# Layer 0's feed-forward network in one pass: seven block products for the latent tokens, down sums per F-tile

## The chip, the core and the metric

The kernel runs on one core of a Trainium2 chip. A core has a matrix engine (PE, whose weight loads the profile lists as PEld), a vector engine (DVE), a scalar engine (ACT), a general engine (POOL) and a queue engine (SP) that issues nearly all DMAs here. Each engine works through its own instructions in program order; semaphores make one wait for another. The metric is device time in microseconds of one execution; three executions of the kernel before gave 1770.62, 1772.52 and 1773.2.

## The reference

Two layers act on 512 latent rows `x` and 256 context rows `ctx`, D = 1024, in fp32. What matters here is the second half of layer 0, for both streams:

```
mx = s_c @ mod_w[l] + mod_b[l]           # six parts of 1024: shift, scale, gate, twice
gate, up = jnp.split(h @ w_in, 2, axis=-1)        # w_in: 1024 x 5632
swiglu   = (jax.nn.silu(gate) * up) @ w_out       # w_out: 2816 x 1024
x   = x   + gx2 * swiglu(rms(x)   * (1 + scx2) + shx2)
ctx = ctx + gc2 * swiglu(rms(ctx) * (1 + scc2) + shc2)
```

The hidden width 2816 is 22 F-tiles of 128. Layer 1 does the same for the latent rows alone, after its own attention.

## The kernel before, in words

**Every product is three.** An fp32 operand is split into a high part in the PE's format (an ACT cast) and a rest (a DVE or POOL subtraction); hi·hi, hi·lo and lo·hi are summed in PSUM.

**Layer 0's FFN** is `ffn`, from 427.9 us of the trace, its last down product at 1003.9 us. It takes the F-tiles in pairs. Per F-tile, gate and up each run over 8 K-tiles of 128 and three passes, and each of these 48 steps is one matmul over the 512 latent columns and one over the 256 context columns (L814, in `half`). ACT takes Silu of the gate (L842), DVE multiplies it by the up (L844), ACT and DVE split the result (L445, L446). Weights arrive raw by SP in two buffers, ACT casts them (L334) and DVE subtracts (L335). The down product of a pair is twelve groups (6 row tiles of 128 by 2 halves of 512 columns), each six matmuls into one of four PSUM banks (L869 to L871). After each group `residual` multiplies the bank by the gate row (L439) and adds it to the rows (L440), both on DVE. The last four F-tiles' downs are done together at the end.

**Layer 1's modulation** (24 chunks of 256 columns for one or two streams, 32 chunk-and-stream units in all) is worked out in the same stretch, by `mod_chunks_by_pool`: ACT scales the raw weights (L213), POOL adds them up (L214 to L219), and PE sums over partitions: a row product per unit (`modrow`, L224) and small products that turn the rows into columns (`modcol`, L232).

**Layer 1's FFN** is already done in blocks (`ffn_by_blocks`): the 512 latent columns and the K dimension are halved, and seven products of quarter size, each 12 matmuls of 256 columns, stand in the place of eight, with sums of weight blocks on POOL ahead and sums of results on DVE behind. All its instructions are recorded through one helper, so the trace gives them one line, L886. It sums each pair's down groups in four banks.

**Order.** In layer 0's `ffn` a scheduler places the instructions; it slips down groups between the gate and up matmuls. In the block code the instructions keep program order on each engine (`Pinned`).

Of the kernel before, what the change touches and what calls it, by code (L numbers as in the profile page):

```python
# [18 lines left out]
P = 128  # L19
# [18 lines left out]
MODS1 = (2, 2, 2, 2, 2, 3, 3, 4, 4, 0)  # L38
# [3 lines left out]
C_N = C_S4 + 4  # L42
# [21 lines left out]
def backbone(es: ExitStack, tc: tile.TileContext, x, c, ctx, c_ctx, mod_w, mod_b, norm_mix_w, norm_ffn_w,  # L64
# [132 lines left out]
    def mod_chunks_by_pool(chunks, pool):  # L197

        width = 256
        all_accs = []  # L200
        for l, part, n, streams in chunks:
            c0 = part * D + n * width
            accs = [pool.tile([P, width], F32, name="ma", tag="ma", bufs=4) for _ in range(streams)]
            for pc in range(2):
                w = pool.tile([P, 4, width], F32, name="modw", tag="mw", bufs=2)
                nc.sync.dma_start(
                    w, mod_w[l, pc * 4 * P:(pc + 1) * 4 * P, c0:c0 + width].rearrange("(j p) n -> p j n", p=P))
                for i, acc in reversed(list(enumerate(accs))):

                    pr = pool.tile([P, 4, width], F32, name="modp", tag="mp", bufs=1) if i else w  # L210
                    for k in range(4):
                        kk = 8 * i + 4 * pc + k
                        nc.scalar.activation(pr[:, k], w[:, k], AF.Copy, scale=cols[:, kk:kk + 1])  # L213
                    nc.gpsimd.tensor_add(pr[:, 0:2], pr[:, 0:2], pr[:, 2:4])  # L214
                    if pc == 0:
                        nc.gpsimd.tensor_add(acc, pr[:, 0], pr[:, 1])
                    else:
                        nc.gpsimd.tensor_add(pr[:, 0], pr[:, 0], pr[:, 1])
                        nc.gpsimd.tensor_add(acc, acc, pr[:, 0])  # L219
            all_accs.extend(accs)  # L220
        ps = tr_tile("modrow", [P, width])

        for j, acc in enumerate(all_accs):
            nc.tensor.matmul(ps[32 * j:32 * j + 32, :], cst[:, C_ONE:C_ONE + 32], acc, start=True, stop=True,  # L224
                             tile_position=(0, 32 * j))
# [1457 lines left out]
```

## Time and profile before

| | |
|---|---|
| median of three executions | 1772.52 us |
| profiled execution | 1773.26 us, its span 1771.4 us |
| mean granted PE clock | 0.99 |
| PE busy in the span | 1696.1 us (96%) |
| DVE, ACT, POOL busy | 1066.9, 852.4, 822.4 us |
| layer 0's FFN, first gate matmul to last down | 427.9 to 1003.9 us |

Times within the profile are microseconds from the start of the span. A group row gives line, engine, operation, what it writes and reads, shape and count; then total busy time and mean ns of one; then idle time ahead of it and what ended it. A row of the timeline gives start, length, engine, line and operation, and in brackets the engine's idle time before it and its releaser. [...]

### The profile page before, as it was taken

The page shows a single profiled execution, that of the slowest core. Times are in us where ns is not written, and L with a number is a line of the kernel's source. Part 1 is how long each engine was busy: PE and PEld are TensorE (multiplying, and loading weights), DVE is VectorE, ACT ScalarE, POOL GpSimd, SP SyncE. Part 2 cuts the span into 40 slices and gives each one's busy share as a digit, 9 for nine tenths or more (in the row PEclk, how much of TensorE's full clock was granted, in tenths as well). Part 3 has the DMA queues.
Part 4 walks back from the last instruction along what each step waited for, and adds up shares of the span by engine and source line. Part 5 has one row for each costly group of instructions (what it writes and reads, how often), then busy time and mean ns, then how long its engine had stood idle before and what let it go on. Part 6 is the DMA issues. An engine that isn't in the chain of part 4 may idle for free. (4 is left out here: it accounts for less than half of the span.)

```text
span 1771.4 us, 28187 instructions
## 1 busy us (share of the span) xinstructions
PE 1696.1 (96%) x10606; PEld 1471.0 (83%) x10606; DVE 1066.9 (60%) x1891; ACT 852.4 (48%) x1841; POOL 822.4 (46%) x1087
## 2 busy tenths in 40 slices
PE   6999999989999999999999999999988999999998
PEld 3887777767888888888888889999986798999997
DVE  4776555444365565554552665666664478877777
ACT  6556565443354444433332466666664345444441
POOL 2753333422054443312230657767772247777770
PEclk8999999999999999999999999999998999999999
DMA  9212233303443334433332211111122325333332
GB/s 319 55 43 73 84 96 108 107 25 119 143 144 97 105 108 155 131 110 108 105 119 62 94 37 36 37 36 51 43 84 83 96 72 161 92 95 107 107 96 95
DMA packets 176168, 169.96 MB, mean 96 GB/s; under 512 B 16608, under 2 KB 162592, under 8 KB 176032
## 3 DMA queue, kind: packets, MB, share of 16 engines
q1 hardware_dynamic: 175680, 167.96, 30.8%
q8 instruction: 83, 1.36, 0.3%
q14 instruction: 53, 0.43, 0.1%
q10 hardware_dynamic: 352, 0.21, 0.0%
HBM read 161.82 MB, written 6.32 MB: 95 GB/s over the span
## 5 line engine op out<-in xcount | busy, mean ns | idle before, releaser
L432 PE MATMUL inps<-wih,hT 128*128 128x384 f32 x384 | 132.9, 346 | 2.1 <-ACT qkv L630 2.0
L439 DVE TENSOR_TENSOR dps<-dps,g 128x512 f32<-128x512 f32 x128 | 87.8, 696 | 72.0 <-PE dps L871 57.6
L434 PE MATMUL inps<-wih,hT 128*128 128x384 f32 x384 | 130.8, 341 | 0.0
L433 PE MATMUL inps<-wil,hT 128*128 128x384 f32 x384 | 130.7, 340 | 0.0
L814 PE MATMUL pg<-hT,wgh 128*128 128x512 f32 x352 | 129.8, 392 | 0.0
L814 PE MATMUL pu<-hT,wuh 128*128 128x512 f32 x352 | 129.4, 391 | 0.4 <-DVE x L440 0.4
L213 ACT ACTIVATE modw<-modw,cols 128x256 f32<-128x256 f32 x192 | 82.0, 498 | 84.1 <-DMA modw<-in_mod_w_dram 80.4
L869 PE MATMUL dps<-wdh,hdh 128*128 128x512 f32 x264 | 106.3, 404 | 1.6 <-DVE x L440 1.6
L870 PE MATMUL dps<-wdl,hdh 128*128 128x512 f32 x264 | 104.5, 396 | 0.0
L871 PE MATMUL dps<-wdh,hdl 128*128 128x512 f32 x264 | 101.8, 396 | 0.0
L214 POOL TENSOR_TENSOR modw<-modw 128x512 f32<-128x512 f32 x48 | 62.1, 1294 | 84.5 <-ACT modw L213 84.5
L814 PE MATMUL pg<-hTc,wgh 128*128 128x256 f32 x352 | 98.1, 282 | 2.7 <-ACT hTc L308 2.4
L814 PE MATMUL pu<-hTc,wuh 128*128 128x256 f32 x352 | 97.8, 282 | 0.0
L321 POOL TENSOR_TENSOR wil<-wir,wih 128x256 fp32r<-128x256 f32 x84 | 68.2, 839 | 62.7 <-ACT wih L334 50.0
L886 PE MATMUL pg<-hT,wbh 128*128 128x256 f32 (+1 forms) x464 | 88.6, 288 | 1.6 <-DVE pg L886 1.6
L886 POOL TENSOR_TENSOR wbl<-ws,wbh 128x256 fp32r<-128x256 f32 x72 | 58.8, 847 | 64.2 <-PE pu L886 54.3
L440 DVE TENSOR_TENSOR x<-x,dps 128x512 f32<-128x512 f32 x128 | 85.2, 682 | 2.3
L552 ACT ACTIVATE Pt<-sc,nm 128x256 f32<-128x256 f32 (+3 forms) x96 | 68.0, 712 | 38.1 <-DVE nm L548 14.7
L886 POOL TENSOR_TENSOR ws<-wr 128x256 f32<-128x256 f32 x72 | 77.1, 1092 | 12.6 <-DMA wr<-in_ffn_w_in_dram 12.6
L886 PEld LDWEIGHTS pg<-hT,wbh 128*128 128x128 f32 x464 | 74.0, 188 | 6.2 <-DVE pg L886 1.8
L814 PEld LDWEIGHTS pg<-hT,wgh 128*128 128x128 f32 x352 | 66.0, 188 | 14.9 <-ACT sg L842 0.4
L814 PEld LDWEIGHTS pu<-hT,wuh 128*128 128x128 f32 x352 | 66.0, 188 | 14.9 <-issue 0.8
(332 smaller groups left out, 5507.1 us busy)
## 6 DMA issues: line engine op xcount, KB each, us to landing
modw<-in_mod_w_dram SPq DMA_DIRECT2D x96, 512.0 KB, 4.4
wdr<-in_ffn_w_out_dram SPq DMA_DIRECT2D x44, 512.0 KB, 3.7
wr<-in_ffn_w_in_dram SPq DMA_DIRECT2D x44, 512.0 KB, 5.2
wir<-in_od_w_in_dram SPq DMA_DIRECT2D x96, 128.0 KB, 2.3
wgr<-in_ffn_w_in_dram SPq DMA_DIRECT2D x22, 512.0 KB, 4.3
wur<-in_ffn_w_in_dram SPq DMA_DIRECT2D x22, 512.0 KB, 3.5
x<-in_x_dram SPq DMA_DIRECT2D x8, 512.0 KB, 6.8
wir<-in_ev_w_in_dram SPq DMA_DIRECT2D x16, 256.0 KB, 2.7
```

Of the source, the lines that this page charges most:

```text
L213: nc.scalar.activation(pr[:, k], w[:, k], AF.Copy, scale=cols[:, kk:kk + 1])
L321: nc.gpsimd.tensor_sub(lo[c], raw[c], hi[c])
L432: nc.tensor.matmul(ps, hs[0][:, k, :], a, start=k == 0, stop=False)
L433: nc.tensor.matmul(ps, hs[0][:, k, :], b, start=False, stop=False)
L434: nc.tensor.matmul(ps, hs[1][:, k, :], a, start=False, stop=k == KT - 1)
L439: nc.vector.tensor_mul(tmp, ps, g[:, n * 512:(n + 1) * 512])
L440: eng.tensor_add(xt[:, n * 512:(n + 1) * 512], xt[:, n * 512:(n + 1) * 512], tmp)
L814: nc.tensor.matmul(ps[:, s0:s1], a, cols_T(b, s0, s1)[:, k, :], start=k == 0 and q == 0, stop=k == KT - 1 and q == 2)
L869: nc.tensor.matmul(ps, hh, a, start=j == 0, stop=False)
L870: nc.tensor.matmul(ps, hh, b, start=False, stop=False)
L871: nc.tensor.matmul(ps, hl, a, start=False, stop=j == nj - 1)
L886: return tc.keep_in_program_order(op(*args, **kw))
```

## The change

Layer 0's FFN becomes `ffn_mixed`, one pass over F-tiles.

- **The first two F-tiles** stay conventional. Meanwhile SP writes all rows to DRAM (the latent ones into the output buffer), and DVE and POOL form the sums of activation blocks. ACT copies this pair's down sums over the rows in SBUF, so that the rows then hold bare sums of the down products.
- **F-tiles 2 to 21** use seven block products of 12 matmuls for the latent tokens (`product`, `four`: `r2`, `r1`, `r3`, `a11`, `a12`, `a22`, `r4`), and 48 matmuls of 256 columns for context's gate and up (`gate_up`).
- **Down sums** are made per F-tile: twelve groups of three matmuls over three banks in turn (`acc0`, `acc1`, `tr0`), each followed by one DVE add into the rows. In tile f stand groups 0 to 7 of tile f-1 and groups 8 to 11 of tile f-2. The fourth bank, `tr1`, holds context's gate and up and the modulation's sums. The last three F-tiles' downs end the pass, with the gate on the sum of all.
- **Gate and rows** come in at the end: tiles 20 and 21 make the gate rows through DRAM, `resumed` multiplies the sums by the gate and adds the rows read back.
- **Layer 1's modulation**: 16 pairs of units, one per tile from tile 4 to 19: four raw loads (`load`), 16 scalings (`scale`), six POOL adds (`sum`), four row matmuls (`rows`), two column matmuls (`columns`). The raw tiles share two buffers with the raw down weights.

All of it from tile 2 on is pinned to program order, under one line, L761. Product, silu, split and gating are as before; the engines' orders ahead of this FFN are unchanged, and in layer 1 ACT, DVE and POOL rows shift a little in the attention. The core of the diff (the sums for the weights, the generators for this layer's own gate part, the end cases of tiles 20 and 21, and the closing of memory pools are left out):

```diff
-MODS1 = (2, 2, 2, 2, 2, 3, 3, 4, 4, 0)
...
-    def mod_chunks_by_pool(chunks, pool):
...
-    def ffn(l, xs, ntok, wp, fp, done, mods=()):
...
+    def ffn_mixed(xs, w_down, w_up, fp, turn_over, new_rows, done):
...
+        def hidden(f, s0, s1, gate, up, sg):
+            hi, lo = (z[:, s0:s1] for z in hid[f])
+            act.activation(sg, gate, AF.Silu)
+            yield
+            dve.tensor_mul(up, sg, up)
+            act.copy(hi, up)
+            yield
+            dve.tensor_sub(lo, up, f32(hi))
...
+        def down_bank(name="dps"):
+            nonlocal bank
+            bank = (bank + 1) % 3
+            return p_1.tile([P, 512], F32, name=name, tag=("acc0", "acc1", "tr0")[bank])
+
+        def group(fs, t, n, keep=False):
+            ps = down_bank()
+            for f in fs:
+                down_part(ps, f, t, n, f == fs[0], f == fs[-1])
+            yield
+            acc = xs[t][:, n * 512:(n + 1) * 512]
+            if keep:
+                act.copy(acc, ps)
+            else:
+                dve.tensor_add(acc, acc, ps)
+
+        def groups(fs, k0, k1, keep=False):
+            some = [group(fs, t, n, keep) for t, n in order[k0:k1]]
+            for g in some:
+                next(g)
+            return some
...
+            def split_last(self):
+                self.t4 = b12
+                act.copy(b12[0], self.f4)
+                dve.tensor_sub(b12[1], self.f4, f32(b12[0]))
...
+        names = ("r2", "r1", "r3", "a11", "a12", "a22", "a21", "r4")
...
+        def hi():
+            if todo:
+                w, n = todo.pop(0)
+                w.w[n] = [blocks.tile([P, half, P], F32R, name="wb" + z, tag="wb" + z, bufs=9) for z in "hl"]
+                act.copy(w.w[n][0], getattr(w, n))
+                made.append((w.w[n], getattr(w, n), n in ("r1", "r2")))
+
+        def lo():
+            if made:
+                (h, t), raw, by_pool = made.pop(0)
+                if by_pool:
+                    for k in range(0, half, 2):
+                        pool.tensor_sub(t[:, k:k + 2], raw[:, k:k + 2], f32(h)[:, k:k + 2])
+                else:
+                    dve.tensor_sub(t, raw, f32(h))
...
+        class Tile:
+
+            def __init__(self, f, w):
+                self.f, self.w = f, w.w
+                self.ps = [banks.tile([P, SEQ], F32, name=n, tag=n) for n in ("pu", "pg")]
+                (self.e, self.b), (self.a, self.c) = ((p[:, :cols], p[:, cols:]) for p in self.ps)
...
+            def four(self):
+                self.quv = three()
+                self.q, self.u, self.v = (self.quv[:, i * cols:(i + 1) * cols] for i in range(3))
+                act.copy(self.q, self.a)
+                dve.tensor_add(self.u, self.b, self.q)
+                dve.tensor_add(self.v, self.c, self.u)
+                dve.tensor_add(self.b, self.e, self.v)
+                dve.tensor_add(self.u, self.e, self.u)
+
+            def gate_up(self, up):
+                if not up:
+                    self.both = tr_tile("cgu", [P, 2, ctx_cols], one=1)
+                for k, n in enumerate(("a21", "a22") if up else ("a11", "a12")):
+                    product(self.both[:, up], self.w[n], ctx_rows[k], k == 0, k == 1)
...
+            def __init__(self):
+                self.pairs = [[(part, n, i) for i in range(2)] for part in range(2) for n in range(4)] + \
+                    [[(part, n + i, 0) for i in range(2)] for part in range(2, 6) for n in (0, 2)]
+                self.now, self.before, self.loads = None, None, []
...
+            def load(self):
+                if self.now:
+                    part, n, _ = self.now[len(self.loads) // 2]
+                    pc, c0 = len(self.loads) % 2, part * D + n * 256
+                    w = raw_tile([P, 4, 256], "modw")
+                    nc.sync.dma_start(
+                        w, mod_w[1, pc * 4 * P:(pc + 1) * 4 * P, c0:c0 + 256].rearrange("(j p) n -> p j n", p=P))
+                    self.loads.append(w)
...
+                    for k in range(4):
+                        kk = 8 * i + 4 * pc + k
+                        act.activation(w[:, k], w[:, k], AF.Copy, scale=cond[:, kk:kk + 1])
...
+                    if s % 2 == 0:
+                        pool.tensor_add(acc, w[:, :512], w[:, 512:])
+                    else:
+                        pool.tensor_add(w[:, :512], w[:, :512], w[:, 512:])
+                        pool.tensor_add(acc, acc, w[:, :512])
...
+            def rows(self):
+                if self.before:
+                    ps = tr_tile("modrow", [P, 256], one=1)
+                    for j in range(4):
+                        pe.matmul(ps[32 * j:32 * j + 32, :], cst[:, C_ONE:C_ONE + 32],
+                                  self.acc[:, j // 2, j % 2 * 256:j % 2 * 256 + 256], start=True, stop=True,
+                                  tile_position=(0, 32 * j))
...
+                    ps = tr_tile("modcol", [P, 2, 2], one=1)
+                    for b in range(2):
+                        pe.matmul(ps[:, b, :], self.r[:, b * P:(b + 1) * P], cst[:, C_S22:C_S22 + 2],
+                                  start=True, stop=True)
...
+        def resumed(t, eng):
+            xr = raw_tile([P, D], "xr")
+            nc.sync.dma_start(xr, out[0, t * P:(t + 1) * P, :] if t < NTX else kept[t])
+            yield
+            eng.tensor_mul(xs[t], xs[t], gates[t // NTX])
+            yield
+            eng.tensor_add(xs[t], xs[t], xr)
...
+        for j in range(2):
+            ps = [p_sc.tile([P, 1024], F32, name=name, tag="sc")[:, :TOK] for name in ("pg", "pu")]
+            for sg in ([[s] for s in segs] if j == 0 else [segs]):
+                for w, z in zip((wg, wu), ps):
+                    first_half(j, w, z, [sg])
...
+        kept = {t: new_rows(t) for t in range(NTX, NT)}
+        for t in range(NT):
+            nc.sync.dma_start(out[0, t * P:(t + 1) * P, :] if t < NTX else kept[t], xs[t])
...
+        end(hidden(0, 0, TOK, *first[0], three()))
+        tt.split(0, 1)
+        w2.sums3()
+        w2.sums4()
+        rest = hidden(1, 0, TOK, *first[1], three())
+        next(rest)
+        tt.split_last()
+        end(rest)
...
+        gs = groups((0, 1), 0, 2, True)
+        for k in range(5):
+            lo()
+            hi()
+            if k % 2:
+                for g in gs:
+                    end(g)
+                gs = groups((0, 1), k + 1, k + 3, True)
...
+        def by_blocks(f, w, nxt, after, last, own):
+            t = Tile(f, w)
+            dn = down(f)
+            next(dn)
+            fs = (0, 1) if f == 2 else (f - 2,)
+            do_a = f != 3 and f < NF - 1
+            do_b = 2 < f < NF - 2
+
...
+            mods.turn(4 <= f < NF - 2)
+            mods.load()
+            t.product("r2")
...
+            if last:
+                next(last)
+            gs = some(8, 10)
+            hi()
+            hi()
...
+            ends(gs)
+            t.product("r1")
+            lo()
+            if last:
...
+            lo()
+            hi()
+            lo()
+            gs = some(10, 12)
+            mods.rows()
+            next(dn)
+            ends(gs)
+            t.product("r3")
+            mods.columns()
+            mods.scale(0)
...
+            if nxt:
+                nxt.sums4()
+            mods.sum(0)
+            end(dn)
+            mods.load()
...
+            gs = some(0, 2)
+            hi()
+            t.product("a11")
+            mods.load()
+            t.four()
+            ends(gs)
...
+            gs = some(2, 4)
+            lo()
+            hi()
+            hidden_tiles(f)
+            t.gate_up(0)
+            rest = hidden(f, SEQ, TOK, t.both[:, 0], t.both[:, 1], ctx_room("sgc"))
+            mods.scale(1)
+            mods.sum(1)
+            next(rest)
+            mods.load()
+            ends(gs)
+            lo()
...
+            gs = some(4, 5)
+            hi()
+            t.product("a12")
+            ends(gs)
+            gs = some(5, 6)
+            dve.tensor_add(t.a, t.a, t.q)
...
+            lo()
+            hi()
+            mods.scale(2)
+            mods.sum(2)
+            t.product("a22")
+            ends(gs)
+            dve.tensor_add(t.e, t.e, t.u)
...
+            gs = some(6, 7)
+            lo()
+            if after:
+                after.sums2()
+            mods.scale(3)
+            mods.sum(3)
+            t.gate_up(1)
+            ends(gs)
+            next(rest)
+            gs = some(7, 8)
+            hi()
+            end(rest)
+            t.product("r4")
+            ends(gs)
+            lo()
+            if f == 2:
+                next(own)
+            dve.tensor_add(t.c, t.c, t.v)
+            last = hidden(f, 0, SEQ, t.ps[1], t.ps[0], t.quv[:, :SEQ])
+            next(last)
...
+        fs = tuple(range(NF - 3, NF))
+        order = [(t, n) for t in CTX_FIRST for n in range(2)]
+        open_ = [p_1.tile([P, 512], F32, name="dps", tag=f"acc{i}") for i in range(2)] + \
+            [banks.tile([P, SEQ], F32, name=n, tag=n) for n in ("pu", "pg")]
+        for ps, (t, n) in zip(open_, order):
+            for f in fs[:2]:
+                down_part(ps, f, t, n, f == fs[0], False)
+        end(last)
+        for i, (t, n) in enumerate(order):
+            ps = open_[i] if i < 4 else acc_tile("dps", one=i % 2)
+            for f in fs[2 * (i < 4):]:
+                down_part(ps, f, t, n, f == fs[0], f == fs[-1])
+            residual(xs[t], ps, gates[t // NTX], n)
+            done(t, n)
...
-        norm_hT(t, xs[t], 1, 0, fp.pool, (("mw", 2), ("mp", 1)))
...
+        norm_hT(t, xs[t], 1, 0, None, room=room)```

Three places show the order. **First, PE at the down products.** Before, in the second pair: `modrow` are the modulation's rows, `dps` a down group's bank, `pg` a gate, `hTc` context's activations. The scheduler puts a group between gate matmuls.

```order
L871 MATMUL dps_5708<-wdh_5400,hdl_5512 128x512
L224 MATMUL modrow_5688<-ma_5620,cst_72 32x256 [waits DVE_49,Pool_49]
L224 MATMUL modrow_5688<-ma_5621,cst_72 32x256
L224 MATMUL modrow_5688<-ma_5654,cst_72 32x256 [waits Pool_49]
L224 MATMUL modrow_5688<-ma_5655,cst_72 32x256
L869 MATMUL dps_5708<-wdh_5406,hdh_5616 128x512 [waits Activation_49]
L870 MATMUL dps_5708<-wdl_5407,hdh_5616 128x512
L871 MATMUL dps_5708<-wdh_5406,hdl_5617 128x512
L814 MATMUL pg_5843<-hTc1_4657,wgh_5815 128x256
L814 MATMUL pg_5843<-hT0_110,wgl_5816 128x512
```

The change, a tile in the middle of the pass, from groups 0 and 1 to the product `a11` (into `pg`):

```order
L761 MATMUL modcol_7873<-cst_72,modr_7854 128x2
L761 MATMUL dps_7891<-wdh_7541,hdh_7621 128x512 [waits DVE_49]
L761 MATMUL dps_7891<-wdl_7542,hdh_7621 128x512
L761 MATMUL dps_7891<-wdh_7541,hdl_7622 128x512 [waits DVE_49]
L761 MATMUL dps_7895<-wdh_7541,hdh_7621 128x512 [waits DVE_49]
L761 MATMUL dps_7895<-wdl_7542,hdh_7621 128x512
L761 MATMUL dps_7895<-wdh_7541,hdl_7622 128x512
L761 MATMUL pg_7782<-hT0_110,wbh_7618 128x256
```

and, ten matmuls further, from the last of `a11` through groups 2 and 3 to context's gate (`cgu`):

```order
L761 MATMUL pg_7782<-hT0_110,wbl_7619 128x256
L761 MATMUL dps_7924<-wdh_7541,hdh_7621 128x512 [waits DVE_49]
L761 MATMUL dps_7924<-wdl_7542,hdh_7621 128x512
L761 MATMUL dps_7924<-wdh_7541,hdl_7622 128x512
L761 MATMUL dps_7928<-wdh_7541,hdh_7621 128x512 [waits DVE_49]
L761 MATMUL dps_7928<-wdl_7542,hdh_7621 128x512
L761 MATMUL dps_7928<-wdh_7541,hdl_7622 128x512
L761 MATMUL cgu_7938<-hTc0_4656,wbh_7618 128x256 [waits PE_49]
```

With three banks in turn, group 3 (`dps_7928`) takes the bank of group 0 (`dps_7891`); only `a11` and group 2 stand between them.

**Second, DVE at the same place.** `quv` holds the values q, u and v of `four`; q is ACT's copy of `a11`'s result, and ACT writes it into `quv_7916` (order of ACT: `L761 COPY quv_7916<-pg_7782`).

```order
L761 TENSOR_TENSOR wdl_7857<-wdr_7783,wdh_7856 128x512
L761 TENSOR_TENSOR quv_7916<-pu_7781,quv_7916 128x256 [waits Activation_49]
L761 TENSOR_TENSOR quv_7916<-pg_7782,quv_7916 128x256 [waits DVE_49]
L761 TENSOR_TENSOR pu_7781<-pu_7781,quv_7916 128x256 [waits DVE_49]
L761 TENSOR_TENSOR quv_7916<-pu_7781,quv_7916 128x256 [waits DVE_49]
L761 TENSOR_TENSOR x0_4046<-x0_4046,dps_7891 128x512 [waits PE_49]
L761 TENSOR_TENSOR x0_4046<-x0_4046,dps_7895 128x512 [waits PE_49]
L761 TENSOR_TENSOR wbl_7900<-ws_7799,wbh_7899 128x512 [waits Pool_49]
L761 TENSOR_TENSOR x1_4203<-x1_4203,dps_7924 128x512 [waits PE_49]
L761 TENSOR_TENSOR x1_4203<-x1_4203,dps_7928 128x512 [waits PE_49]
```

The adds that empty the banks of groups 0 and 1 (`x0`) stand behind the four `quv` adds. The same order holds in tiles 3 to 19, 17 of them; tile 2 has no groups 0 to 7.

**Third, DVE where the two conventional tiles end.** `tf` are raw sums of activation blocks, `hT1_111` the low half of the activations.

```order
L761 TENSOR_TENSOR tf3_4921<-tf3_4921,hT1_111 128x1024
L761 TENSOR_TENSOR pu_4963<-quv_5192,pu_4963 128x768 [waits PE_49,Activation_49]
L761 TENSOR_TENSOR hdl_5061<-pu_4963,hdh_5060 128x768 [waits Activation_49]
L761 TENSOR_TENSOR t2l_5173<-tf1_5175,t2h_5172 128x1024 [waits Activation_49]
L761 TENSOR_TENSOR t1l_5171<-tf0_5174,t1h_5170 128x1024 [waits Activation_49]
L761 TENSOR_TENSOR hT1_111<-tf3_4921,hT0_110 128x4x256 [waits DVE_49,Activation_49,Pool_49]
L761 TENSOR_TENSOR pu_5063<-quv_5207,pu_5063 128x768 [waits DVE_49,PE_49]
L761 TENSOR_TENSOR hdl_5161<-pu_5063,hdh_5160 128x768 [waits Activation_49]
```

`split_last` writes the block sum `t4` over a quarter of the activations (`hT0`, then `hT1`), which the second conventional tile reads to its end (ACT's row: `L761 CAST hT0_110<-tf3_4921 128x4x256 [waits PE_49,Pool_49]`). Behind it on DVE stand the second tile's product (`pu_5063`) and split (`hdl_5161`), which its down groups read.

More of the change, by code (lines that the diff above doesn't have):

```diff
@@ L195, in mod_chunk @@
         add_mod(l, part, k0, k1, sums, 2)
-    def mod_chunks_by_pool(chunks, pool):
[L199 to L225, printed above, removed]
-        m = len(all_accs)
-        r = all_accs[0]
-        nc.scalar.copy(r[:32 * m], ps[:32 * m])
-        ps = tr_tile("modcol", [P, 2, m])
-        for b in range(2):
-            nc.tensor.matmul(ps[:, b, :], r[:32 * m, b * P:(b + 1) * P], cst[:32 * m, C_S4:C_S4 + m],
-                             start=True, stop=True)
-        i = 0
-        for l, part, n, streams in chunks:
-            add_mod(l, part, 2 * n, 2 * n + 2, ps[:, :, i:i + streams], streams)
-            i += streams
@@ L239, in add_mod @@
-    def add_mod(l, part, k0, k1, ps, streams):
+    def add_mod(l, part, k0, k1, ps, streams, eng=nc.vector):
         mc = modc[l][:, part, k0:k1, 0:streams]
-        nc.vector.tensor_tensor(mc, ps, bc(bcol[:, l, part, k0:k1], 2, streams), ALU.add)
+        eng.tensor_tensor(mc, ps, bc(bcol[:, l, part, k0:k1], 2, streams), ALU.add)
         if part in (1, 4):
@@ L252, in gate_row @@
         nc.tensor.transpose(ps, modc[l][:, part, :, i], ident)
-        row = small.tile([KT, P], F32, name="grow", tag="grow", bufs=2)
+        row = small.tile([KT, P], F32, name="grow", tag="grow", bufs=1)
         nc.vector.tensor_copy(row, ps)
@@ L1478, in done0 @@
             nc.sync.dma_start(out[0, t * P:(t + 1) * P, :], xs[t])
-        norm_hT(t, xs[t], 1, 0, fp.pool, (("mw", 2), ("mp", 1)))
-    rest = [(1, part, n, 2 if part < 2 else 1) for part in range(6) for n in range(4)]
-    mods = [[(0, 5, n) for n in range(4)]]
-    for n in MODS1:
-        mods.append(rest[:n])
-        rest = rest[n:]
-    ffn(0, xs, NT, ws, fp.pool, done0, mods)
-    ws[1].close()
-    ws[0].close()
+        room = [fp.pool.tile([P, KT, P], F32, name="nh", tag=tag) for tag in (("t1l", "t2h")[t % 2], "t2l")]
+        norm_hT(t, xs[t], 1, 0, None, room=room)
+    fb_pool = None
+    ffn_mixed(xs, ws[0].pool, ws[1].pool, fp.pool, turn_over,
+              lambda t: dram.tile([P, D], F32, name=f"cx{t}", tag=f"cx{t}"), done0)
+    fb_pool.__exit__(None, None, None)
+    sc_pool = score_banks()
+    p_sc = sc_pool.__enter__()
+    nb.pop().close()
+    ws.pop().close()
+    wp = Pool("mw1", "right")
     tab = Pool("tab1", "right")
```

374 lines of the change are left out of this document (282 added, 92 removed).

## The prediction

> **What bounds the kernel now.** The page's first two sections were read first:
>
> ```profile
> PE 1696.1 (96%) x10606; PEld 1471.0 (83%) x10606; DVE 1066.9 (60%) x1891; ACT 852.4 (48%) x1841; POOL 822.4 (46%) x1087
> PEclk8999999999999999999999999999998999999999
> ```
>
> PE is busy for 96% of the span at nearly full clock, so a pass over layer 0's FFN costs what its matmuls cost, and any pause of PE is paid in full. The table by stretches says the same of the stage itself, and the second row shows layer 1's FFN, where the block products already run:
>
> ```profile
> 530.00:580.00 50.00, 50.00 (x271) 41.71 (x270) 27.89 (x37) 22.89 (x46) 21.36 (x22) 1.00 0.31 95
> 1535.00:1595.00 60.00, 60.00 (x421) 55.74 (x420) 46.96 (x78) 25.35 (x44) 44.47 (x48) 1.00 0.33 96
> ```
>
> PE (second column) never rests in either, while DVE, ACT and POOL (fourth to sixth) have room. What a matmul costs is read from starts, in PE's timeline and in the chain of waits (start, length, engine, tile, count):
>
> ```profile
> 954.95 0.39 PE L814 MATMUL pg<-hT,wgh 128*128 128x512 f32 x1
> 955.30 0.39 PE L814 MATMUL pg<-hT,wgl 128*128 128x512 f32 x1
> ...
> 1477.41 1.40 PE dps L886 x6
> 1478.80 1.40 PE pg L886 x12
> ```
>
> A step of gate or up (512 and 256 columns) takes 0.35 us, a matmul of 512 columns 1.40/6 = 0.234, one of 256 columns 1.40/12 = 0.117.
>
> **The change part by part.**
>
> *Matmuls.* Before, an F-tile costs 48 × 0.351 = 16.85 plus its downs, 36 × 0.234 = 8.42: 25.27. After, a block tile costs 84 × 0.117 = 9.83, context's 48 × 0.117 = 5.62, and the same 8.42: 23.87. Twenty tiles: **−28.1**.
>
> *Layer 1's modulation.* The same 32 units go through PE, but in 16 batches of four row matmuls in the place of 8 full ones, and 16 batches of two column matmuls in the place of nine:
>
> ```profile
> 576.04 0.64 PE L224 MATMUL modrow<-ma,cst 128*32 128x256 f32 x8
> 576.61 0.50 PE L869 MATMUL dps<-wdh,hdh 128*128 128x512 f32 x1
> ...
> 580.77 0.50 PE L232 MATMUL modcol<-cst,ma 128*128 128x4 f32 x4
> 581.13 0.48 PE L869 MATMUL dps<-wdh,hdh 128*128 128x512 f32 x1
> 581.45 0.40 PE L870 MATMUL dps<-wdl,hdh 128*128 128x512 f32 x1
> ```
>
> (x8 and x4 are two passes each.) A row batch takes 0.57; a column batch 0.36 and 0.09 by which the next matmul is late, 0.45. So 8 × 0.57 + 7 × 0.45 = **+7.7**. The scalings and POOL adds are off PE's path (the loads below).
>
> *The bank of group 3.* This is the part that decides. In tiles 3 to 19 group 3 writes the bank that group 0 filled, so it waits for DVE's add of group 0, and that add stands behind the four `quv` adds, the first of which needs ACT's copy of product `a11`, the product that PE has only just ended. PE has nothing to put into the time but group 2, and being in order it cannot go on to context's gate. The rows for each step, from layer 1's FFN where the same operations run:
>
> ```profile
> L886 ACT COPY q<-pg x17: 376/379/394, 1477.0 to 1723.8; 128x256 f32<-128x256 f32 x17
> ...
> 1565.43 0.28 PE L886 MATMUL pg<-hT,wbl 128*128 128x256 f32 x1
> ...
> 1565.75 0.43 DVE L886 TENSOR_TENSOR pg<-pg,v 128x256 f32<-128x256 f32 x1 [0.31 <-PE pg L886]
> ...
> 1568.46 0.59 ACT L886 CAST hdh<-pu 128x512 fp32r<-128x512 f32 x1 [1.08 <-DVE pu L886]
> ...
> 1569.09 0.69 DVE L886 TENSOR_TENSOR hdl<-pu,hdh 128x512 fp32r<-128x512 f32 x1 [0.65 <-ACT hdh L886]
> ...
> 1574.24 0.42 DVE L886 TENSOR_TENSOR pu<-pu,v 128x256 f32<-128x256 f32 x1
> 1574.70 0.42 DVE L886 TENSOR_TENSOR w<-pu,u 128x256 f32<-128x256 f32 x1
> 1575.04 1.12 DVE L886 TENSOR_TENSOR wdl<-wdr,wdh 128x512 fp32r<-128x512 f32 x1
> ...
> L886 DVE TENSOR_TENSOR x<-x,dps 128x512 f32<-128x512 f32 x64 | 43.6, 681 | 23.4 <-PE dps L886 23.4
> ```
>
> Counted from the start of `a11`'s last matmul: a reader of its result starts 0.32 later (1565.43 to 1565.75); the copy takes 0.38; DVE follows ACT after 0.04 (1568.46 + 0.59 to 1569.09), so u starts at 0.74. A dependent add follows after 0.46 (1574.24 to 1574.70), an independent operation after 0.34. Three dependent steps and one of 0.34 put group 0's add at 2.46; with its 0.68 and 0.04 to PE, group 3 may start at 3.18. Unhindered it would start after `a11`'s last matmul and group 2, at 0.117 + 3 × 0.234 = 0.82. PE rests for 2.36 us, 17 times: **+40.1**. If all the steps follow each other like independent ones it is 2.0 (34), with the copy or u held up behind other work on ACT or DVE 2.6 or more (44). Queued behind the wait are group 3, context's gate and all that follows; nothing later wins it back, since PE is the bound.
>
> *The engines beside PE.* Layer 1's tile is 84 × 0.117 + 24 × 0.234 = 15.4 us; by its window row DVE spends 12.1 of these, POOL 11.4, ACT 6.5. The new tile adds on DVE eight adds of 0.68 and context's multiplication and split (about 0.9), on POOL six adds and on ACT sixteen scalings:
>
> ```profile
> L214 POOL TENSOR_TENSOR modw<-modw 128x512 f32<-128x512 f32 x48 | 62.1, 1294 | 84.5 <-ACT modw L213 84.5
> L213 ACT ACTIVATE modw<-modw,cols 128x256 f32<-128x256 f32 x192 | 82.0, 498 | 84.1 <-DMA modw<-in_mod_w_dram 80.4
> ```
>
> So DVE about 18.5 to 20, POOL 19.2, ACT 15 to 17 of a tile of over 24: none is the bound.
>
> *Where the conventional tiles end.* `split_last` may write only after the second tile's last matmul; behind it stand the second tile's multiplication and split, and behind those its down groups:
>
> ```profile
> L334 ACT CAST wuh<-wur 128x1024 fp32r<-128x1024 f32 x22 | 23.1, 1048 | 54.0 <-PE pu L814 46.9 <-DMA wur<-in_ffn_w_in_dram 7.1
> L335 DVE TENSOR_TENSOR wul<-wur,wuh 128x1024 fp32r<-128x1024 f32 x22 | 30.5, 1388 | 28.3 <-ACT wuh L334 28.3
> L844 DVE TENSOR_TENSOR pu<-sg,pu 128x768 f32<-128x768 f32 x22 | 21.2, 962 | 78.2 <-PE pu L814 72.3 <-ACT sg L842 5.9
> L446 DVE TENSOR_TENSOR hdl<-pu,hdh 128x768 fp32r<-128x768 f32 x22 | 20.9, 952 | 14.1 <-ACT hdh L445 14.1
> L445 ACT CAST hdh<-pu 128x768 fp32r<-128x768 f32 x22 | 17.5, 797 | 70.7 <-DVE pu L844 70.7
> ```
>
> 1.05 + 1.39 + 0.96 + 0.80 + 0.95 = 5.15, less the 0.70 of the three matmuls that need only the first tile, is 4.45; the copies of this pair's banks on ACT, between weight casts, are put at 1.5. **+6** (4 to 9).
>
> *The end.* The gate rows come through DRAM in tiles 20 and 21, which have little else for PE to do, and the last downs need them:
>
> ```profile
> L439 DVE TENSOR_TENSOR dps<-dps,g 128x512 f32<-128x512 f32 x128 | 87.8, 696 | 72.0 <-PE dps L871 57.6 <-DMA g<-gmem 8.1 <-PE dps L886 5.5
> ```
>
> DVE once waited 8.1 us for such a gate before. At the end three F-tiles are summed in the place of four, 12 × 9 × 0.234 = 25 us of PE against 34, over the same twelve residuals and norms. I take **+4** (0 to 8).
>
> *The clock.* A pause may cost more than itself. The stretches of 4 us show it both ways, with PE's rows inside them:
>
> ```profile
> 440.00:444.00 4.00, 1.88 (x13) 1.42 (x11) 1.64 (x4) 2.03 (x5) 0.00 (x0) 1.00 0.15 48
> 444.00:448.00 4.00, 3.46 (x27) 3.25 (x28) 1.29 (x2) 0.79 (x2) 0.00 (x0) 1.00 0.01 4
> ...
> 1412.00:1416.00 4.00, 1.83 (x13) 1.28 (x11) 3.55 (x8) 3.58 (x8) 0.00 (x0) 0.99 1.17 303
> 1416.00:1420.00 4.00, 4.00 (x21) 4.00 (x22) 3.81 (x6) 4.00 (x10) 2.82 (x3) 0.58 0.71 231
> ```
>
> ```profile
> 444.32 0.39 PE L814 MATMUL pg<-hTc,wgh 128*128 128x256 f32 x1 [2.44 <-ACT hTc L308]
> ```
>
> After the pause of 2.44 us the granted clock stayed at 1.00; after 2.17 us of idle between 1412 and 1416 it was 0.58 for 4 us, a loss of 0.42 × 4 = 1.7. Per pause the cost lies between 0 and 1.7; I take 0.5, since a third of such cases seems a fair share of the two, and 17 pauses make **+8.5** (0 to 29). [...]
>
> *Sum.* −28.1 + 7.7 + 40.1 + 6 + 4 + 8.5 = +38.2. The profiled execution took 1773.26, which gives 1811.5; it stands 0.7 above the median of the runs, so **1811**.
>
> **The rivals.**
>
> *The bank is no obstacle* (the other side). The order names the engine that group 3 waits for, not the instruction. If the add in question is an older one, or group 0's bank is free in time, the pause goes, and its clock with it: 1773.3 − 28.1 + 7.7 + 6 + 4 = 1762.9, by the median 1762. It decides from 0.6 us a tile on: 17 × 0.6 = 10.4 is what the other terms leave. For it speaks that layer 1's FFN, of the same build, has PE at 60.00 of 60.00, but it has four banks there, and four groups a tile. Against it: three banks in turn, so group 3 can only mean group 0. Chance 0.12.
>
> *The clock holds.* All pauses behave like that at 444: 1811 − 8.5 = 1803. Chance 0.17. [...]
>
> *The clock falls each time*, as at 1416: 1811 + 20.4 = 1832. Chance 0.13.
>
> *The raw buffers become the bound.* Five raw tiles per F-tile (one down weight, four of modulation) share two buffers, and each must land, be cast or scaled, and be added up before its buffer is loaded again:
>
> ```profile
> modw<-in_mod_w_dram SPq DMA_DIRECT2D x48, 512.0 KB, 4.3
> wdr<-in_ffn_w_out_dram SPq DMA_DIRECT2D x18, 512.0 KB, 6.0
> ```
>
> With these landings: 6.0 + 1.05 + 2 × 0.89 (layer 1's split of down weights) = 8.8 for the down tile; 4.3 + 4 × 0.5 + 1.3 or 2.6 for the others, 33 for four. Over two buffers that is 20.9 us a tile, below 27 (23.87, the modulation's 1.0 and the pause). If all land in 6.0 it is 24.3, and with 1.7 us of queueing per tile behind casts on ACT and sums on POOL 28.6: then ACT stalls at a scaling, with context's cast and the next weights' casts behind it, and PE runs at 28.6, some 1.3 us more for 16 tiles, 21 in all: 1832. Chance 0.13.
>
> **How the numbers follow.** The forecast has the remaining 0.45. Its own range, by the bounds above, is 1798 to 1826. The range given, 1785 to 1840, takes in all but the first rival and the far tail of the last two. A difference of 0.2%, 3.5 us, is about what a measurement of this kernel tells from none. Faster is the first rival when the pause is nearly gone, 0.09; within 0.2% is the same rival with a pause of half a microsecond, 0.03; slower has the rest, 0.88.
>
> **What would show it.** In each of tiles 3 to 19 PE has one idle time of about 2.4 us before group 3, released by DVE's add of `x`, and the same group's row sums to some 40 us; PE's starts inside a tile keep 0.117 and 0.234; a tile takes about 27 us. Were the largest idle time before scalings on ACT, released by DMA, and a tile 28 us or more, the raw buffers are the bound. A tile of 25 us without that idle time would show the first rival. The clock's part is read in stretches of 4 us after the pauses: 1.00 there takes 8.5 off the sum. The forecast is wrong if PE's idle time before group 3 is under 1 us.

## The result and the profile after

The changed kernel takes 1858.78 us (median of four, 1857.12 to 1859.14) against 1772.86 (four): a ratio of 1.0483, 95% interval 1.0465 to 1.0502, so 86 us slower. The side was forecast; the size, 1811 in a range of 1785 to 1840, was not. The profiled execution has 1857.12 us and a span of 1855.2.

Page of the change, busy time and PE's clock:

```profile
PE 1700.9 (92%) x11418; PEld 1501.9 (81%) x11418; DVE 1193.3 (64%) x2178; ACT 924.3 (50%) x2044; POOL 1000.1 (54%) x1270
PEclk8999999999999999999999779999999999999999
```

PE is as busy as before in microseconds, 1700.9 against 1696.1, in a span that is 84 longer: the time went into pauses and a slower clock, not into work (at a granted clock of 0.50 a matmul of 512 columns counts with 0.63 us in the place of 0.40). The clock now drops in two slices after the middle, at 1020 to 1110 us. The table of PE's waits between 420 and 1110 us (line, releaser, total, times, longest) names the pauses. Before:

```profile
PE pg L814 <- ACT hTc L308: 2.4, 1, 2.4
PE dps L869 <- DVE x L440: 1.6, 2, 1.1
```

After:

```profile
PE dps L761 <- DVE x L761: 38.0, 17, 2.3
PE npt L264 <- POOL nh L258: 26.4, 5, 6.2
PE inps L398 <- POOL wil L286: 11.3, 2, 10.3
PE pg L1283 <- ACT hTc L273: 5.3, 1, 5.3
PE cgu L761 <- DVE grow L761: 1.8, 1, 1.8
PE dps L761 <- ACT hdh L761: 1.2, 1, 1.2
PE dps L761 <- ACT x L761: 1.0, 1, 1.0
```

The first row is the pause that the prediction worked out: 17 times before group 3, 2.25 us each (1.95 in tile 3). One of them in PE's timeline, between the last matmul of group 2 and the first of group 3:

```profile
603.92 0.40 PE L761 MATMUL dps<-wdh,hdl 128*128 128x512 f32 x1
606.57 0.50 PE L761 MATMUL dps<-wdh,hdh 128*128 128x512 f32 x1 [2.25 <-DVE x L761]
```

The next two rows of the table stand where the prediction had put +4: `npt` are the transposes in the norm of the finished rows for layer 1, `inps` is layer 1's first projection, `wil` its split weights. The stretches of 20 us there, for the change (PE's busy time second, its clock third from the end):

```profile
1000.00:1020.00 20.00, 18.23 (x155) 18.01 (x154) 17.00 (x26) 4.20 (x8) 2.41 (x1) 1.00 0.42 131
1020.00:1040.00 20.00, 13.59 (x64) 11.05 (x63) 12.85 (x19) 5.58 (x11) 10.01 (x6) 0.83 0.18 61
1040.00:1060.00 20.00, 9.94 (x37) 8.31 (x38) 8.55 (x17) 6.19 (x13) 3.73 (x6) 0.72 0.06 26
1060.00:1080.00 20.00, 11.41 (x42) 8.82 (x40) 9.82 (x17) 6.99 (x14) 2.50 (x5) 0.84 0.13 53
1080.00:1100.00 20.00, 8.31 (x30) 6.93 (x31) 6.78 (x15) 4.75 (x9) 9.36 (x15) 0.67 0.09 32
```

and before, in the last downs and the start of layer 1:

```profile
980.00:1000.00 20.00, 19.51 (x98) 15.84 (x97) 15.30 (x27) 9.90 (x20) 15.89 (x23) 1.00 0.33 105
1000.00:1020.00 20.00, 20.00 (x126) 18.39 (x125) 13.95 (x27) 11.37 (x28) 10.58 (x19) 1.00 0.24 85
```

From 1020 to 1100 us PE is busy for 43 of 80 us, in part at a low clock, and no other engine for as long. The timeline of one row tile shows why:

```profile
1051.70 0.39 PE L761 MATMUL dps<-wdh,hdl 128*128 128x512 f32 x1
...
1052.86 0.69 DVE L405 TENSOR_TENSOR x<-x,dps 128x512 f32<-128x512 f32 x1
1053.64 1.06 ACT L256 ACTIVATE nh<-x 128x1024 f32<-128x1024 f32 x1 [3.54 <-DVE x L405]
1054.87 0.19 POOL L166 TENSOR_SCALAR rs_n<-nss 128x1 f32<-128x1 f32 x1 [9.75 <-ACT nh L256]
1055.14 0.55 POOL L167 TENSOR_TENSOR rs_n<-rs_n,neghalf 128x1 f32<-128x1 f32 x1
1055.80 1.12 POOL L258 TENSOR_SCALAR nh<-x,rs_n 128x1024 f32<-128x1024 f32 x1
...
1056.97 1.97 PE L264 MATMUL npt<-cst,nh 128*128 128x128 f32 x8 [4.89 <-POOL nh L258]
1058.59 0.77 PE L761 MATMUL dps<-wdh,hdh 128*128 128x512 f32 x1
1059.16 0.63 PE L761 MATMUL dps<-wdl,hdh 128*128 128x512 f32 x1
1059.59 0.63 PE L761 MATMUL dps<-wdh,hdl 128*128 128x512 f32 x1
```

A row tile's last down, its residual on DVE, the square on ACT, the scaling on POOL and the transposes on PE follow each other, and the next row tile's downs, whose operands are all there, stand behind the transposes. So the engines take turns, and after each pause PE's matmuls follow at 0.43 us in the place of 0.234 (1059.59 on 1059.16), with the granted clock at 0.50.

From layer 0's first gate matmul to its last down matmul, by the starts of PE's rows, it was 428.2 to 1010.0, 582 us; now it is 430.4 to 1088.5, 658 us. (The 1003.9 given for the kernel before is not its last down: the last row of L871 starts at 1010.0.)

```profile
L871 PE MATMUL dps<-wdh,hdl x264: 388/394/481, 470.3 to 1010.0; 128*128 128x512 f32 x132
```

That is 76 of the 84 us. Another 2.3 lie ahead of the first gate, and 5 behind the last down, 767 us in the place of 761: the wait of 10.3 us for layer 1's split weights stands there.

### The profile page after: what moved, and what is told of

Same layout as the page of the kernel before. It is cut to its first block, busy times and chain, and to the rows that moved or that the text cites. A ratio compares the mean times of both kernels' runs of the same rounds, so it can differ in the third digit from the quotient of the medians.

```text
span 1855.2 us, 30669 instructions
## 1 busy us (share of the span) xinstructions
PE 1700.9 (92%) x11418; PEld 1501.9 (81%) x11418; DVE 1193.3 (64%) x2178; ACT 924.3 (50%) x2044; POOL 1000.1 (54%) x1270
## 5 line engine op out<-in xcount | busy, mean ns | idle before, releaser
L761 PE MATMUL dps<-wdh,hdh 128*128 128x512 f32 x434 | 177.8, 410 | 40.2 <-DVE x L761 38.0
L761 DVE TENSOR_TENSOR x<-x,dps 128x512 f32<-128x512 f32 x268 | 178.2, 681 | 49.6 <-PE dps L761 49.2
L761 POOL TENSOR_TENSOR wbl<-ws,wbh 128x256 fp32r<-128x256 f32 x152 | 118.9, 812 | 141.3 <-ACT wbh L761 76.7
L761 PE MATMUL pg<-hT,wbh 128*128 128x256 f32 (+1 forms) x944 | 176.2, 284 | 1.5 <-DVE pg L761 1.5
L761 PE MATMUL dps<-wdl,hdh 128*128 128x512 f32 x434 | 173.3, 399 | 0.0
L761 PE MATMUL dps<-wdh,hdl 128*128 128x512 f32 x434 | 172.6, 398 | 0.3 <-DVE hdl L761 0.3
L761 PEld LDWEIGHTS pg<-hT,wbh 128*128 128x128 f32 x944 | 150.7, 188 | 10.7 <-DVE pg L761 1.9
L761 POOL TENSOR_TENSOR ws<-wr 128x256 f32<-128x256 f32 x152 | 143.1, 961 | 16.4 <-DMA wr<-in_ffn_w_in_dram 13.2
L761 DVE TENSOR_TENSOR wbl<-wr,wbh 128x512 fp32r<-128x512 f32 x142 | 133.6, 943 | 6.0 <-ACT wbh L761 5.4
L761 PE MATMUL pg<-hT,wbl 128*128 128x256 f32 (+1 forms) x472 | 133.7, 283 | 0.0
L761 PEld LDWEIGHTS dps<-wdh,hdh 128*128 128x128 f32 x434 | 83.1, 191 | 58.7 <-DVE x L761 45.5
L398 PE MATMUL inps<-wil,hT 128*128 128x384 f32 x384 | 130.5, 340 | 0.0
L761 ACT ACTIVATE modw<-modw,cols 128x256 f32<-128x256 f32 x256 | 108.5, 498 | 27.6 <-DMA modw<-in_mod_w_dram 19.3
L761 PE MATMUL cgu<-hTc,wbh 128*128 128x256 f32 x640 | 118.8, 287 | 1.8 <-DVE grow L761 1.8
L761 ACT CAST wbh<-wr 128x512 fp32r<-128x512 f32 x142 | 87.5, 620 | 47.9 <-PE pg L761 31.1
L761 ACT CAST wbh<-ws 128x512 fp32r<-128x512 f32 x152 | 87.4, 624 | 43.8 <-PE pg L761 31.9
L761 PEld LDWEIGHTS cgu<-hTc,wbh 128*128 128x128 f32 x640 | 103.7, 195 | 5.4 <-DVE grow L761 2.0
L761 PEld LDWEIGHTS dps<-wdh,hdl 128*128 128x128 f32 x434 | 82.6, 190 | 20.5 <-DVE hdl L761 0.7
L761 PE MATMUL cgu<-hTc,wbl 128*128 128x256 f32 x320 | 91.5, 286 | 0.0
L761 PEld LDWEIGHTS dps<-wdl,hdh 128*128 128x128 f32 x434 | 83.1, 192 | 9.5
```

What stands on the lines that cost most here:

```text
L398: nc.tensor.matmul(ps, hs[0][:, k, :], b, start=False, stop=False)
L761: return tc.keep_in_program_order(op(*args, **kw))
```

## The experiments

All ratios are to runs of the kernel before on the same chip; their medians are 1772.28 for e1 to e4, 1773.39 for e5 to e8, 1773.74 for e9 to e11 and 1772.63 for e12. Between these groups the ratios compare better than the times.

**The two places, apart and together.** `e1_adds_first` turns two lines round in each block tile:

```diff
-            t.four()
             ends(gs)
+            t.four()
```

> Only change: in each block tile the adds that empty the banks of groups 0 and 1 stand ahead of the four sums on DVE. The theory of the bank (the pause before group 3 is real and nothing stands behind it): PE's 17 idle times of 2.25 us and the three slower stretches of clock after them (1.55 us each in the tile period) go, 38 + 5 = 43 us less than the change: about 1816, a tile about 25.3 us. Rival: the raw buffers or another engine are the next bound close behind, and a tile stays above 26.5 us: 1835 or more, with idle time of PE in front of something else in tiles 4 to 19.

Measured: 1814.73, ratio 1.0242 (1.0227 to 1.0258), 44 us less than the change. Of the 17 waits two short ones are left:

```profile
PE dps L761 <- DVE x L761: 1.6, 2, 1.0
```

By the starts of their first products, tiles 5 to 19 were 27.66 us apart and three of them 29.2; now they are 25.15, but for the two that hold these waits (26.0 and 26.4). So a pause costs 2.51: 2.25 idle, 0.16 by which the row before it lasts longer than matmuls follow each other (0.40 against 0.234), and 0.10 by which the second matmul behind it comes late (606.90 on 606.57). The bank is shown, and no other engine stood close behind.

`e2_end_free` gives the last downs back to the scheduler:

```diff
             for f in fs[2 * (i < 4):]:
-                down_part(ps, f, t, n, f == fs[0], f == fs[-1])
+                down_part(ps, f, t, n, f == fs[0], f == fs[-1], nc.tensor)
```

> Only change: the matmuls of the last downs are no longer held in program order, so that the scheduler may put them ahead of the transposes of an earlier row tile's norm. The theory of the order at the end: PE's five idle times of 4.9 to 6.2 us before the transposes (26.4 us) and the half clock after each (some 1.5 us each) go, 25 to 34 us less: 1825 to 1834. Rival: the chain of residual, norm and split takes its 10 to 12 us per row tile in any order, since each row tile waits for banks that the residual empties; then the time falls by less than 10 us, and PE waits for DVE's add of x instead. A wait of about 10 us for layer 1's first split weights is expected to stay in either case.

Measured: 1824.15, ratio 1.0297 (1.0282 to 1.0313), 34.6 us less. The five waits for `nh` are gone; what is left of them is

```profile
PE npt L264 <- ACT nh L269: 6.8, 2, 6.2
```

so PE's order was the cause, not the length of the chain; one wait of 6.2 stays, which e10 takes up below. The wait of 10.3 us for layer 1's split weights went too, which was not expected.

> Both edits. If the two places do not touch each other the gains add up: 43 and 25 to 34 us, so 1782 to 1791, still slower than the kernel before. Rival: one hides the other in part (a shorter block stage brings the gate rows and layer 1's loads later against PE), above 1795.

Measured: 1776.33, ratio 1.0029 (1.0018 to 1.0040), 82.4 us less, against 78.7 for the sum of the two. They are additive within 4 us and explain all but some 4 of the 86.

**The start, by the prediction's step.** `e4_split_later`, on top of both:

```diff
-        tt.split_last()
         end(rest)
+        tt.split_last()
```

> Both edits, and the split of the block sum t4 stands behind the second conventional tile's product and split. By the prediction's working it takes 2.4 us off the start (1.05 of ACT and 1.39 of DVE ahead of the second tile's product); by the trace of the change, where PE waited only 1.2 and 0.3 us there, 1.5 us. Rival: it changes nothing, since ACT's copies of the bank set that stretch.

Measured: 1779.79, ratio 1.0048 (1.0031 to 1.0064): no gain, and 3 us more that are not explained. PE's waits at that place are the same as in the change (1.2 for `hdh`, 1.1 for `x`). The rows of DVE in the change show why:

```profile
471.17 1.22 DVE L761 TENSOR_TENSOR hT<-tf,hT 128x1024 fp32r<-128x1024 f32 x1 [7.67 <-issue]
474.26 0.96 DVE L761 TENSOR_TENSOR pu<-quv,pu 128x768 f32<-128x768 f32 x1 [1.86 <-PE pu L1283]
```

The split (`hT`) is done at 472.4, and the product (`pu`) comes 1.86 us later, when PE has ended the tile. The quarter of the activations that the split writes holds K-tiles 0 to 3, which the tile's last product has read when it is half done; the second tile does not read it to its end. So the split was not in the chain at all, and the prediction's 4.45 us is not what PE waits for there.

**What is left: queue, modulation, gates.** `e5_stores_later` pins the writes of the rows (`Pinned(nc.sync).dma_start(...)`), on top of both.

> The two edits (adds first, free end), and the writes of the rows to DRAM are held behind the loads of the first weights in SP's queue. The theory that these writes, each waiting for a residual, hold up the weight loads queued behind them: the pass begins some 2.3 us earlier, the idle time of 5.4 us before context's first gate falls to about the 2.4 of the kernel before, and the clock does not fall after it: 4 to 8 us less than with the two edits alone (1776.3), 1768 to 1772. Rival: DVE's sums of activation blocks hold up context's norm, then the idle time stays at 5 us and no more than 2 us is gained, 1774 to 1776.

Measured: 1775.79, ratio 1.0017 (1.0006 to 1.0029). The idle time before context's first gate stays at 5.2: the writes are not the cause, as the rival said.

`e6_mods_batched`, on top of both, lets POOL add the two halves of each unit, and two tiles share a batch:

```diff
-                    w, acc = self.loads[s].rearrange("p k n -> p (k n)"), self.acc[:, s // 2]
-                    if s % 2 == 0:
-                        pool.tensor_add(acc, w[:, :512], w[:, 512:])
+                    w, acc = self.loads[s].rearrange("p k n -> p (k n)"), self.acc[:, 2 * len(self.past) + s // 2]
+                    pool.tensor_add(w[:, :512], w[:, :512], w[:, 512:])
+                    if s % 2 == 0:
+                        pool.tensor_add(acc, w[:, :256], w[:, 256:512])
...
-                                  self.acc[:, j // 2, j % 2 * 256:j % 2 * 256 + 256], start=True, stop=True,
+                                  self.acc[:, j], start=True, stop=True,
```

> The two edits, and layer 1's modulation goes through PE in eight batches of four row and two column products (two tiles share one, POOL adds the two halves of each unit first) in the place of sixteen. By the prediction's term of 7.7 us: 1768 to 1769; by the tile period without idle time (about 25.2 against 23.9 of matmuls alone) up to 10 us: 1766. Rival: the further adds make POOL the bound of a tile, and the time stays or rises.

Measured: 1771.17, ratio 0.9985 (0.9974 to 0.9996). Tiles alternate between 25.15 and 23.93 us: a batch costs 1.22, and a tile without one is at the 23.87 that its matmuls alone were worked out to take. Eight batches fewer are 9.8 us; from tile 2 to tile 21 4.7 of them arrive (463.3 us against 468.1 in e3), because five tiles now wait 0.3 to 1.5 us for DVE's add of `x`. In the whole time it is 5 us by the medians, 8 by the ratios.

`e7_all` has the four edits:

> All four edits. If they add up 1758 to 1764, faster than the kernel before by 8 to 14 us. Rival: they overlap in part and it comes to 1766 to 1772, no difference from the kernel before that the runs can tell.

Measured: 1771.53, ratio 0.9993 (0.9982 to 1.0005). The rival holds: the later writes add nothing. `e8_gates_early` also sends both gate rows off in tile 20:

> As the four edits, and both gate rows leave for DRAM in tile 20, so that context's gate in tile 21 need not wait for the bank of the second one: the idle times of 1.8 and 0.4 us there become 0.4 in all, 1.5 to 2 us less. Rival: no change, since the last residuals set the end.

Measured: 1774.56, ratio 1.0000 (0.9987 to 1.0013), no gain. The wait of 1.8 us for `grow` is gone, and in its place stands

```profile
PE pg L761 <- DVE quv L761: 2.6, 1, 2.6
```

**The context norm and the rope tables.** `e9_norm_first` stands on e6 and queues the sums of activation blocks (`make`: seven steps of DVE and three of POOL) behind the norm:

```diff
-        tt.make()
+        with tc.issue_after(turn["norm"]):
+            tt.make()
```

> Adds first, free end, modulation in batches, and DVE's sums of activation blocks queued behind the last step of context's norm. The theory that these sums (1.2 us each, between the steps of the norm) cause the longer idle time before context's first gate: 5.5 us falls to 2.5 to 3.5, and the clock after it holds; 3 to 6 us less than with the first three edits (1771.2): 1765 to 1768. Rival: the norm's own chain over ACT and PE sets it, and nothing changes; or the sums come late for the first block product, and PE waits there instead.

Measured: 1773.35, ratio 1.0005 (0.9996 to 1.0014), no gain. The theory on the norm holds, and so does the rival in kind, though it named another place: PE's waits are

```profile
PE pu L1283 <- DVE hdl L761: 5.6, 1, 5.6
...
PE pg L1283 <- ACT hTc L273: 2.4, 1, 2.4
```

The 5.5 us fell to the 2.4 of the kernel before, and the sums then held up the split of the first conventional tile, whose banks the second one needs (not the first block product, as the rival had it).

`e10_tables_early` stands on e6, too. There POOL's rope products came between two norms, after a load that waits for the last down to free its memory (rows of e6: SP, POOL, PE):

```profile
1000.37 0.34 SPq L332 DMA_DIRECT2D rw<-in_od_qn_dram  x1
...
1003.69 6.41 POOL L344 TENSOR_TENSOR rt<-rp,rw 128x256 f32<-128x256 f32 x8 [1.40 <-DMA rw<-in_od_kn_dram]
...
1010.31 1.94 PE L264 MATMUL npt<-cst,nh 128*128 128x128 f32 x8 [6.19 <-ACT nh L269]
```

The edit puts `rw` into a tile of the FFN that is free earlier:

```diff
-        w = pool.tile([P, 2, 2, HD], F32, name="rw", tag="rw")
+        w = room or pool.tile([P, 2, 2, HD], F32, name="rw", tag="rw")
...
-    tabs = head_tables(tab.pool, od_qn[0], od_kn[0], 2, 2)
+    tabs = head_tables(tab.pool, od_qn[0], od_kn[0], 2, 2,
+                       fp.pool.tile([P, 2, 2, HD], F32, name="rw", tag="sgc"))
```

> Adds first, free end, modulation in batches, and the small rope weights of layer 1 are loaded into a tile that is free after the last block product, not into memory that the last down weights hold. The theory that POOL's eight rope products (6.4 us), released only by that load after the last down, stand ahead of a norm's scaling and of the first split weights: the 6.2 us of PE's idle time before the transposes goes and the clock between 1000 and 1020 us holds, 4 to 10 us less than 1771.2: 1761 to 1767. Rival: without it the transposes wait as long for the residual and norm of the last row tile, 0 to 2 us.

Measured: 1769.95, ratio 0.9982 (0.9973 to 0.9991). The wait of 6.2 us is 1.4 now, and the waits for layer 1's split weights and casts, 3.5 in all in e6, are 8.4: one wait in the place of another, and in time little or nothing.

`e11_both` has e9's and e10's edits together:

> All five edits. If the two add up: 1757 to 1764, 9 to 16 us faster than the kernel before. Rival: 1768 to 1771, no more than the three edits give.

Measured: 1773.23, ratio 1.0001 (0.9992 to 1.0010): the rival, and worse; PE waits 4.0 us for `hdl` here.

`e12_sums_split` is e11 with the sums in two parts: three of DVE's seven steps (and POOL's three) behind the norm, four behind the first conventional tile's product and split. Its call sites, without the division of `make` itself:

```diff
         with tc.issue_after(turn["norm"]):
-            tt.make()
+            tt.make(0)
...
         end(hidden(0, 0, TOK, *first[0], three()))
+        tt.make(1)
```

> Adds first, free end, modulation in batches, early rope weights, and of the sums of activation blocks the first three DVE steps stand behind context's norm, the other four behind the first conventional tile's product and split. Theory from the run before, where all seven stood behind the norm and PE then waited 5.6 us for that tile's split: both waits go, context's first gate waits 2.4 us in the place of 5.4 and the clock after it holds: 3 to 5 us less than 1770: 1765 to 1767. Rival: the sums come late for the split of the first block sums, and PE waits as long before the first block product: 1769 to 1772.

Measured: 1763.44, ratio 0.9957 (0.9941 to 0.9973), some 9 us less than before by the medians and 7.6 by the ratio, and below the forecast; of the kernels here it is the fastest. Context's first gate waits 2.4 us, no wait for `hdl` takes its place, and the clock holds behind it. The same 30 us in e10 and then in e12:

```profile
430.00:460.00 30.00, 24.56 (x128) 21.44 (x128) 22.62 (x28) 12.50 (x21) 13.84 (x8) 0.89 0.29 93
```

```profile
430.00:460.00 30.00, 27.34 (x162) 23.51 (x161) 23.98 (x26) 12.47 (x22) 17.27 (x10) 1.00 0.27 85
```

## Why the prediction was right in its side and wrong in its size

| Term of the sum | predicted | shown |
|---|---|---|
| matmuls of a block tile | 23.87 us | 23.93 (tiles without modulation) |
| modulation through PE | +7.7 | 1.22 a batch, 16 batches: 19.5, where the working had 1.02 and 16.3; so about +11, if the batches before cost what the working gave them |
| the bank of group 3 | 17 × 2.36 = +40.1 | 17 × 2.51 = +42.7 |
| the clock | +8.5 | +4.7 (three tiles longer by 1.55) in the block stage; more at the end, below |
| start | +6 | about +10: pauses of 7.8 us where the kernel before has 2.8, some 3 at half clock behind the longest (0.50 from 447.95 to 454.77), 2.3 by which it begins later |
| end | +4 (0 to 8) | its removal gives 34.6 alone (e2) and 38.4 on top of e1 (e3) |

The shown sizes come to some 80 of the 86 us; the rest is not placed.

**Right:** the bank. Its chain was worked out from layer 1's rows step by step, and its place, number, length and releaser came as forecast; e1 takes it away. The raw buffers are no bound, and the rival "the bank is no obstacle" is refuted.

**Wrong:** the step "The end". It took the last downs as 25 us of PE's work "over the same twelve residuals and norms", and so counted work where order decides. The rows for a better reckoning stand in the trace of the kernel before. The chain of one row tile (0.7 and 0.7 of residual on DVE, 1.25 on ACT, 1.9 on POOL) is some 5 us long, five times; what had hidden it before was a scheduler free to put later downs and layer 1's first projection ahead of the transposes. The change holds the downs in program order, and the prediction named this for the bank ("being in order it cannot go on to context's gate") but did not ask what follows the last tile. There the transposes stand between the down groups in the change's order, and the sum has no term for it. The 26.4 us of pauses, the half clock after each and the 11.3 us in front of layer 1's weights stand in its place; e2 takes 34.6 us of them away and leaves a wait of 6.2.

**The clock.** Three of the 17 pauses were followed by a slower stretch, the mixture that the term of 0.5 each was meant to say; it was put at nearly twice the size. Which three it was is read from the last section's rows. The five pauses at the end, of 4.9 to 6.2 us, were each followed by matmuls of 512 columns at 0.43 us.

**The start.** The two pauses that the working meant are 1.2 and 0.3 us; e4 and the rows beside it show that the split of the block sum, 2.44 of the chain's 5.15, is not in it: it need not wait for the tile's last matmul. What was missed is upstream: DVE's sums of activation blocks (`tf`) slip between the steps of context's norm (`nhc`, L271), and context's first gate waits 5.3 in the place of 2.4, with the granted clock at 0.89 from 430 to 460 us, as in e10.

```profile
445.63 0.40 DVE L271 TENSOR_SCALAR nhc<-npt,aff,modc 128x128 f32<-128x128 f32 x1
445.95 1.21 DVE L761 TENSOR_TENSOR tf<-hT,tf 128x1024 f32<-128x1024 f32 x1
447.09 0.72 DVE L271 TENSOR_SCALAR nhc<-npt,aff,modc 128x128 f32<-128x128 f32 x2
```

e9 and e12 show this; e5 shows that the writes of the rows, a second suspect, do not matter.

**Still open:** why the stage begins 2.3 us later than before (it does so in e5, too, at 430.4, and hardly in e9 and e12, at 428.8 and 428.4), the few us of the sum that are not placed, and the last 4 us by which the two gains together are more than their sum.

## What to carry to other kernels

When a part of a program is pinned to its order, walk through the order to the point where the pinned part ends: a chain that another engine runs between two independent pieces of work costs its full length if the first engine's next instruction is the chain's end (here 4.9 to 6.2 us, five times). For a ring of banks, count which instructions stand between the write and the reuse, and what stands ahead of the emptying instruction on the engine that empties it; turning two lines round was worth 44 us here. A saving in matmuls (28 us by the prediction's sum) shows nothing until both have been done; the best kernel here keeps some 9 us of it. Removing one wait showed the next one behind it in e8, e9 and e10.

## What the runs showed of the hardware

Seventeen pauses, sixteen of 2.25 us and one of 1.95, were not alike in what followed. Two stretches behind a pause of the change, at 606.57 and at 634.23:

```profile
606.57:610.00 3.43, 3.43 (x26) 3.30 (x27) 3.06 (x5) 1.13 (x3) 2.14 (x2) 1.00 0.20 68
```

```profile
636.20:638.20 2.00, 2.00 (x11) 2.00 (x11) 1.03 (x2) 0.00 (x0) 1.92 (x2) 0.50 0.00 0
```

The first keeps its clock, the second falls to a half for 3.41 us (635.68 to 639.09), which is where that tile's 1.55 us come from. What differs is the place of the pause in time. All changes of the granted clock in this trace lie on one grid with steps of 3.41 us (from 430 to 950 us they are at 447.95, 454.77, 635.68, 639.09, 775.62, 779.04, 942.88 and 946.29). The steps of the grid in which these two pauses mostly lie are

```profile
604.96:608.37 3.41, 1.80 (x12) 1.67 (x13) 3.34 (x8) 1.71 (x4) 0.59 (x1) 1.00 0.57 177
632.27:635.68 3.41, 1.45 (x9) 1.32 (x10) 3.34 (x7) 1.71 (x4) 0.28 (x1) 1.00 0.62 207
```

PE is idle for 1.61 us of the first and for 1.96 of the second, and the clock falls at the end of the second. Over the 17 pauses, four put 1.87 us or more into one step, and three of these are followed by a fall; the other 13 put in 1.81 or less, and none is. In e2, with the same 17 waits (38.0 us), the granted clock from 490 to 1000 us was 0.99, as in the change. The prediction's two cases fit: in the kernel before, the pause of 2.44 us lies with some 1.2 in each of two steps and keeps the clock, and the pauses of 1.23 and 0.94 put 2.1 into the step that ends at 1415.9, where it falls. In other stages the clock also fell with less idle time in a step (1.46 at 1040.4 of the kernel before). So, in these tiles, pauses of one length differ in where they lie on the grid, and the three followed by a fall are among the four with the most idle time in one step. That the place decides is the author's reading of these rows; no run moved a pause on purpose.

An elementwise addition of 1024 columns on DVE took 1.21 us while POOL was idle, and 3.27 beside one on POOL, which took 3.28; the addition ahead of it took 1.22, though POOL's began 0.16 us after it did (change, DVE and POOL):

```profile
447.73 1.21 DVE L761 TENSOR_TENSOR tf<-tf,hT 128x1024 f32<-128x1024 f32 x1
...
450.08 1.22 DVE L761 TENSOR_TENSOR tf<-hT,tf 128x1024 f32<-128x1024 f32 x1
451.33 3.27 DVE L761 TENSOR_TENSOR tf<-tf,hT 128x1024 f32<-128x1024 f32 x1
```

```profile
450.24 3.28 POOL L761 TENSOR_TENSOR tf<-hT 128x1024 f32<-128x1024 f32 x1 [8.27 <-DVE hTc L274]
```

In e9, whose edit puts POOL's three steps behind the norm as well, the seven sums in one piece took 16.3 us on DVE (445.87 to 462.14), where seven of 1.21 are 8.5. In e12 two of them took 6.65 us together (from 446.58), beside POOL's three (445.50 to 455.50). That POOL's sums are the reason is argued from these rows, since no run took them away.
